# Windowed attention inside a two-layer encoder: the query split moves to the weight-sum tiles, and probabilities, values and unit ends come one step later

## The chip, the cores and the metric

The kernel runs on one core of one Trainium2 chip. The metric is the device time of one execution in microseconds (us). Engines are named as in the profile: PE (TensorE matmul), PEld (TensorE weight load, which runs beside PE), DVE (VectorE), ACT (ScalarE), POOL (GpSimd) and SP (SyncE, which here only issues DMAs).

## What is computed

Two sequences, 512 and 256 tokens of width 1024, go through two layers with the same weights. Each layer is half a SwiGLU network, a token mixer, and half a SwiGLU network again; layer 0 mixes with a gated linear recurrence, layer 1 with windowed attention. The change touches the attention alone:

```python
def window_gqa_mixer(x, w_qkv, w_o, sinks):        # 16 query heads, 4 key heads, head width 64
    q, k, v = split(x @ w_qkv)
    q, k = rope_partial(q), rope_partial(k)
    ...
    s = einsum('bnqhgd,bnkhd->bnhgqk', qb, kband) * d ** -0.5
    s = where(|kpos - qpos| <= 128, s, -inf)
    m = maximum(max(s), sink)
    p = exp(s - m)
    denom = sum(p) + exp(sink - m)
    o = einsum('bnhgqk,bnkhd->bnqhgd', p / denom, vband)
    return o.reshape(B, T, Hq * d) @ w_o
```

## The kernel before

**Numbers in two parts.** Matmuls run on fp32r operands. An fp32 operand is cast to fp32r (the high part, ACT) and the rest is subtracted (the low part, DVE); a product takes three matmuls (lines 261 to 263). `split` (lines 266, 267) does this for activations, lines 167 and 168 for weights.

**Memory.** Large activations live in an arena (`big`, 21 slots of 6 KB per partition). Weights arrive raw in `wr` tiles through the SP queue (line 152) and leave as `w` tiles. Two further tiles, tag `s3`, hold sums of weight blocks for the feed-forward stages: line 186 loads a block into them, line 142 adds another by a POOL-issued DMA. No attention weight uses them. All matmul outputs go to eight PSUM banks (`ps`).

**The attention stage** (`swa`, line 945) lies between the second layer's two feed-forward halves. It first projects keys and values, then runs 24 units: for each of 4 key heads, the 6 blocks of 128 tokens, each with the 4 query heads of that key head. A unit's steps are the methods of `Unit` (line 1107):

- `query`: splits the rotated query block, 128x256, high part on ACT, low part on DVE (lines 266, 267), into a tile `st`
- `turn`: four PE transposes of `st` (line 943) and one ACT copy of the result to SBUF (line 1132)
- `scores`: two matmuls for each of four heads (lines 1141, 1142), each head followed by one DVE instruction that adds the mask and takes the minimum (line 1144)
- `exps`, `sink`, `denominator`: four ACT exponentials (line 1157), small sums (lines 1163, 1164, 1169), a reciprocal (line 1170) and four POOL multiplications that normalize (line 1173)
- `probs(j)`: for each key block j, four PE transposes (line 1179) and a split of the result on ACT and DVE (lines 266, 267, now to `tA` tiles)
- `values(j)`: two matmuls (lines 1191, 1192) that add up in one bank `po`
- `finish`: an ACT copy (line 1197) and two DVE additions (line 1202) that empty `po`

**What sets the order.** `pipeline` (line 1080) gives each of these calls a step number; unit i starts at step 4i. Between them it puts pieces of the query projection, of the output projection (`wo`, lines 261 to 263), and the splits of finished attention outputs (lines 1016, 1017). The calls are recorded in that order, and a scheduler places the instructions on each engine by that order, their data and the tile slots that are free. On the chip each engine then takes its own list strictly in turn.

Of the kernel before, what the change touches and what calls it, by code (L numbers as in the profile page):

```python
# [10 lines left out]
F32R = mybir.dt.float32r  # L11
# [5 lines left out]
P = 128  # L17
# [11 lines left out]
GQ = 4  # L29
# [19 lines left out]
class Trunk:  # L49
# [1030 lines left out]
    def pipeline(self, units, extra):  # L1080
        events = []

        def at(step, rank, *calls):
            events.append((step, rank, len(events), calls))

        for i, u in enumerate(units):
            t = 4 * i
            at(t - (3 if i else 5), 5, u.query)
            at(t - 2, 3.5, u.turn)
            for h in range(GQ):  # L1090
                at(t + h // 2, 0, lambda u=u, h=h: u.scores(h))
            at(t + 2, 2, u.sink)
            for h in range(GQ):
                at(t + 1 + h // 2, 2, lambda u=u, h=h: u.exps(h))
            at(t + 2, 2, u.denominator)
            for j in range(u.nkb):
                at(t + 6 + j, 1, lambda u=u, j=j: u.probs(j))
                at(t + 8 + j, 4, lambda u=u, j=j: u.values(j))
            at(t + 7 + u.nkb, 4, u.finish)
        for step, call in extra:  # L1100
            at(step, 3, call)
        for _, _, _, calls in sorted(events, key=lambda e: e[:3]):
            for c in calls:
                c()


class Unit:
# [12 lines left out]
    def query(self):  # L1120
        k = self.k
        q = self.q().rearrange("p (h d) -> p h d", d=HD)
        self.st = k.big([P, GQ, P], F32R)
        k.split(q, self.st[:, :, :HD], self.st[:, :, HD:])

    def turn(self):
# [190 lines left out]
```

## Time and profile before

| | us |
|---|---|
| median of 3 runs (2806.42 to 2807.36) | 2807.12 |
| the profiled execution's own time | 2808.21 |
| its span in the profile | 2806.4 |
| PE busy | 2775.5 |
| DVE busy | 2161.0 |
| ACT busy | 1329.5 |
| POOL busy | 372.7 |
| attention units on PE, first score to last score | 2089 to 2263 |

The span runs from the first to the last instruction; the remaining 1.8 us lie around it. Matmuls overlap each other, so a busy PE row does not mean that PE starts matmuls as fast as it can.

### The profile page before, as it was taken

How to read it: one execution, taken by the hardware profiler on the slowest of the kernel's cores; microseconds unless marked ns; L12 is line 12 of the kernel's file. 1: busy time of each engine (PE TensorE's matmuls, PEld its weight loads, DVE VectorE, ACT ScalarE, POOL GpSimd, SP SyncE). 2: the span in 40 equal slices, each digit the busy share in tenths (PEclk: the TensorE clock that was granted, in tenths of full speed). 3: DMA queues.
4: the chain of work that ended last, by engine and by line, in shares of the span. 5: the costliest groups of instructions: out<-in, count | busy, mean ns of one | idle time of the engine just before them, and what ended most of it. 6: DMA issues, size and time to landing. Idle time of an engine off the chain costs nothing.

```text
span 2806.4 us, 40557 instructions
## 1 busy us (share of the span) xinstructions
PE 2775.5 (99%) x15225; PEld 2551.2 (91%) x15225; DVE 2161.0 (77%) x3760; ACT 1329.5 (47%) x2455; POOL 372.7 (13%) x402
## 2 busy tenths in 40 slices
PE   8999999999999999999999999999999899999998
PEld 8999999889899889999999999999887789999998
DVE  8788788477577658878878887887848868878877
ACT  6344444444344436434444644444458755444443
POOL 2111121000000001211111111111002211211111
PEclk9999999999999999999999999999999999999999
DMA  6554464311111133555444355554412113555443
GB/s 175 126 130 120 114 145 125 107 46 38 52 40 31 65 94 83 142 126 131 118 116 121 83 143 129 127 120 113 138 69 76 38 47 82 145 134 127 115 118 108
DMA packets 330101, 291.37 MB, mean 104 GB/s; under 512 B 11608, under 2 KB 257840, under 8 KB 329904
## 3 DMA queue, kind: packets, MB, share of 16 engines
q1 hardware_dynamic: 293920, 212.37, 25.5%
q0 software_dynamic: 31680, 62.93, 13.5%
q10 hardware_dynamic: 4304, 13.49, 1.3%
q8 instruction: 119, 1.95, 0.3%
q14 instruction: 78, 0.64, 0.1%
HBM read 216.39 MB, written 9.44 MB: 80 GB/s over the span
## 4 chain that ended last, share of the span: by engine, by line
PE 95%; ACT 2%; DVE 2%; DMA 0%; POOL 0%; issue 0%; DVEq 0%; ACTq 0%; POOLq 0%
PE ps L437 42%; PE ps L501 20%; PE ps L263 8%; PE ps L261 8%; PE ps L262 8%; PE ps L693 3%; PE ps L797 1%; PE ps L773 1%; PE ps L331 1%; PE ps L1179 1%; ACT big L1157 0%; PE ps L1141 0%; POOL big L1173 0%; PE ps L943 0%; PE ps L1192 0%
## 5 line engine op out<-in xcount | busy, mean ns | idle before, releaser
L437 PE MATMUL ps<-big,w 128*128 128x384 f32 x6720 | 1169.3, 334 | 0.0
L437 PEld LDWEIGHTS ps<-big,w 128*128 128x128 f32 x6720 | 1165.9, 188 | 1.7 <-ACT tA L454 0.2
L200 ACT CAST w<-wr 128x512 fp32r<-128x512 f32 x600 | 417.1, 707 | 680.8 <-PE ps L437 273.3
L501 PE MATMUL ps<-w,big 128*128 128x512 f32 x2520 | 575.3, 389 | 0.0
L501 PEld LDWEIGHTS ps<-w,big 128*128 128x128 f32 x2520 | 472.7, 188 | 97.5
L201 DVE TENSOR_TENSOR w<-wr,w 128x512 fp32r<-128x512 f32 (+1 forms) x520 | 429.6, 830 | 157.8 <-ACT w L200 133.4
L523 DVE SCALAR_TENSOR_TENSOR x<-ps,x 128x512 f32<-128x512 f32 x468 | 301.9, 683 | 10.0 <-PE ps L263 9.9
L142 POOL DMA_DIRECT2D s<-wr x120 | 104.9, 874 | 1504.5 <-DMA wr<-in_ffn_w_dram 646.9
L261 PE MATMUL ps<-w,big 128*128 128x512 f32 x624 | 250.0, 401 | 0.3
L263 PE MATMUL ps<-w,big 128*128 128x512 f32 x624 | 245.2, 393 | 2.1 <-DVE big L1017 1.1
L262 PE MATMUL ps<-w,big 128*128 128x512 f32 x624 | 244.5, 392 | 0.0
L261 PE MATMUL ps<-big,w 128*128 128x384 f32 (+2 forms) x640 | 220.1, 345 | 2.1 <-DVE big L339 1.1
L262 PE MATMUL ps<-big,w 128*128 128x384 f32 (+2 forms) x640 | 216.1, 338 | 0.2
L263 PE MATMUL ps<-big,w 128*128 128x384 f32 (+2 forms) x640 | 215.3, 336 | 0.0
L266 ACT CAST big<-tA 128x384 fp32r<-128x384 f32 x296 | 148.1, 513 | 112.8 <-DVE tA L476 36.2
L267 DVE TENSOR_TENSOR big<-tA,big 128x384 fp32r<-128x384 f32 x296 | 168.2, 579 | 6.7 <-ACT big L266 4.5
L168 DVE TENSOR_TENSOR w<-wr,w 128x1024 fp32r<-128x1024 f32 x92 | 111.8, 1221 | 78.0 <-ACT w L167 72.7
L201 POOL TENSOR_TENSOR w<-wr,w 128x512 fp32r<-128x512 f32 x80 | 134.1, 1676 | 187.8 <-ACT w L200 187.5
L167 ACT CAST w<-wr 128x1024 fp32r<-128x1024 f32 x92 | 96.6, 1052 | 108.8 <-PE ps L262 85.8
L142 POOL DMA_DIRECT2D wr<-wr x100 | 87.7, 877 | 420.6 <-DVE w L201 177.5
L263 PEld LDWEIGHTS ps<-w,big 128*128 128x128 f32 x624 | 117.4, 188 | 28.5 <-DVE big L1017 2.0
L261 PEld LDWEIGHTS ps<-w,big 128*128 128x128 f32 x624 | 117.8, 189 | 22.3 <-ACT w L167 0.3
(175 smaller groups left out, 3276.4 us busy)
## 6 DMA issues: line engine op xcount, KB each, us to landing
wr<-in_ffn_w_dram SPq DMA_DIRECT2D x264, 512.0 KB, 3.9
s<-in_ffn_w_dram SPq DMA_DIRECT2D x120, 256.0 KB, 3.2
s<-wr POOLq DMA_DIRECT2D x120, 256.0 KB, 4.8
wr<-wr POOLq DMA_DIRECT2D x80, 256.0 KB, 3.8
wr<-in_hg_w_in_dram SPq DMA_DIRECT2D x40, 512.0 KB, 3.7
wr<-wr POOLq DMA_DIRECT2D x20, 512.0 KB, 4.6
spill<-x ACTq DMA_DIRECT2D x12, 512.0 KB, 3.3
x<-spill ACTq DMA_DIRECT2D x12, 512.0 KB, 3.2
```

The lines of the kernel that those rows point to most:

```text
L142: self.nc.gpsimd.dma_start(out, src, accum_op=ALU.add)
L168: self.nc.vector.tensor_sub(lo, raw, hi.bitcast(F32))
L200: nc.scalar.copy(h, src)
L201: (eng or nc.vector).tensor_sub(l, src, h.bitcast(F32))
L261: nc.tensor.matmul(out, a[0], b[0], start=first, stop=False)
L262: nc.tensor.matmul(out, a[0], b[1], start=False, stop=False)
L263: nc.tensor.matmul(out, a[1], b[0], start=False, stop=last)
L266: self.nc.scalar.copy(hi, src)
L267: self.nc.vector.tensor_sub(lo, src, hi.bitcast(F32))
L437: self.nc.tensor.matmul(ps, a[x], b[y], start=first and k == 0 and i == 0, stop=k == 3 and i == 2, skip_group_check=True,)
L501: nc.tensor.matmul(ps, a[x], w[y], start=name == chain and kp == 0 and q == 0, stop=kp == 1 and q == 2, skip_group_check=True,)
L523: self.nc.vector.scalar_tensor_tensor(x, ps, c, x, ALU.mult, ALU.add)
```

## The change

Two edits. The tile for the split query comes from the two `s3` tiles, each 512 columns, in place of an arena slot. And in the table of steps, `probs`, `values` and `finish` of each unit move one step later against everything else.

```diff
             for j in range(u.nkb):
-                at(t + 6 + j, 1, lambda u=u, j=j: u.probs(j))
-                at(t + 8 + j, 4, lambda u=u, j=j: u.values(j))
-            at(t + 7 + u.nkb, 4, u.finish)
+                at(t + 7 + j, 1, lambda u=u, j=j: u.probs(j))
+                at(t + 9 + j, 4, lambda u=u, j=j: u.values(j))
+            at(t + 8 + u.nkb, 4, u.finish)
...
-        self.st = k.big([P, GQ, P], F32R)
+        st = k.wp.tile([P, 512], F32R, tag="s3", name=k.name("s3"), bufs=2)
+        self.st = st.rearrange("p (h d) -> p h d", d=P)
         k.split(q, self.st[:, :, :HD], self.st[:, :, HD:])
```

Since a line is added, lines from 1124 on are numbered one higher in the changed kernel (scores 1142 and 1143, probabilities 1180, values 1192 and 1193).

What this does to the engines' lists shows at three places. The first is the DVE list around the low part of unit 21's query (it reads `big_19580`, the rotated queries). Before, it stands behind unit 18's `finish` (L1202), unit 19's first probability split (which writes `tA_20380`) and a weight split (L168):

```order
L1163 TENSOR_TENSOR stat_20329<-stat_20327,nsinks 128x4
L168 TENSOR_TENSOR w_20359<-wr_19809,w_20358 128x1024
L1202 TENSOR_TENSOR big_20368<-ps_20338,tA_20366 64x2x128 x2
L267 TENSOR_TENSOR tA_20380<-ps_20374,tA_20379 128x512
L267 TENSOR_TENSOR big_20371<-big_19580,big_20371 128x4x64
L1169 TENSOR_TENSOR stat_20328<-stat_20328,stat_20329 128x4
L521 TENSOR_TENSOR x_19544<-ps_20351,x_19544 128x512
```

In the changed kernel the same subtraction writes the `s3` tile (printed as `s_3093_20364`):

```order
L1170 TENSOR_TENSOR stat_20139<-stat_20139,stat_20140 128x4
L1171 RECIPROCAL stat_20139<-stat_20139 128x4
L1203 TENSOR_TENSOR big_19806<-ps_20175,tA_20207 64x2x128 x2
L267 TENSOR_TENSOR tA_20217<-ps_20211,tA_20216 128x512
L267 TENSOR_TENSOR s_3093_20364<-big_19580,s_3093_20364 128x4x64
L1145 ISA big_20227,stat_20228<-ps_20231,big_17955,nsinks 128x384
```

There it stands behind unit 16's `finish` and unit 17's first probability split, and ahead of unit 19's first scores: two units earlier.

The second place is the PE list at unit 10, from its query transposes (L943) to its first score. Before, one block of unit 8's probability transposes (L1179) lies between them:

```order
L943 MATMUL ps_19348<-ident_r,big_19320 128x128 x4
L1179 MATMUL ps_19361<-ident_r,big_19189 128x128 x4
L1141 MATMUL ps_19374<-big_17959,tA_19353 128x256
L1142 MATMUL ps_19374<-big_17959,tA_19353 128x256
L1141 MATMUL ps_19378<-big_17959,tA_19353 128x256
L1142 MATMUL ps_19378<-big_17959,tA_19353 128x256
```

In the changed kernel the first score (L1142) follows directly behind these twelve rows:

```order
L943 MATMUL ps_19337<-ident_r,s_2835_19318 128x128 x4
L1192 MATMUL ps_19315<-tA_19286,big_17962 128x512
L1180 MATMUL ps_19346<-ident_r,big_19180 128x128 x4
L261 MATMUL ps_19239<-w_18814,big_17871 128x512
L1193 MATMUL ps_19315<-tA_19287,big_17962 128x512
L1192 MATMUL ps_19315<-tA_19309,big_17962 128x512
L262 MATMUL ps_19239<-w_18815,big_17871 128x512
L263 MATMUL ps_19239<-w_18814,big_17871 128x512
L261 MATMUL ps_19239<-w_18814,big_17872 128x512
L1193 MATMUL ps_19315<-tA_19310,big_17962 128x512
L262 MATMUL ps_19239<-w_18815,big_17872 128x512
L263 MATMUL ps_19239<-w_18814,big_17872 128x512
```

Value matmuls of unit 7 (L1192, L1193) and a stretch of projection now stand between the transposes and the scores.

The third place is the PE list at unit 16, again from its query transposes. `big_19732` before, and `big_19723` after, are unit 14's probabilities. Before:

```order
L943 MATMUL ps_19919<-ident_r,big_19885 128x128 x4
L1179 MATMUL ps_19932<-ident_r,big_19732 128x128 x4
L1141 MATMUL ps_19945<-big_17960,tA_19924 128x256
L1142 MATMUL ps_19945<-big_17960,tA_19924 128x256
L1141 MATMUL ps_19949<-big_17960,tA_19924 128x256
L1142 MATMUL ps_19949<-big_17960,tA_19924 128x256
L1179 MATMUL ps_19953<-ident_r,big_19732 128x128 x4
L1191 MATMUL ps_19980<-tA_19893,big_17962 128x512
L1192 MATMUL ps_19980<-tA_19894,big_17962 128x512
L1141 MATMUL ps_19983<-big_17960,tA_19924 128x256
```

In the changed kernel:

```order
L943 MATMUL ps_19908<-ident_r,s_2977_19883 128x128 x4
L1180 MATMUL ps_19917<-ident_r,big_19723 128x128 x4
L1142 MATMUL ps_19936<-big_17960,tA_19913 128x256
L1143 MATMUL ps_19936<-big_17960,tA_19913 128x256
L1142 MATMUL ps_19940<-big_17960,tA_19913 128x256
L1143 MATMUL ps_19940<-big_17960,tA_19913 128x256
L1180 MATMUL ps_19944<-ident_r,big_19723 128x128 x4
L1142 MATMUL ps_19971<-big_17960,tA_19913 128x256
L1143 MATMUL ps_19971<-big_17960,tA_19913 128x256
L1142 MATMUL ps_19975<-big_17960,tA_19913 128x256
L1143 MATMUL ps_19975<-big_17960,tA_19913 128x256
L1180 MATMUL ps_19979<-ident_r,big_19723 128x128 x4
```

Here the row behind the query transposes is still one block of probability transposes, but it is unit 14's first block where it was the second; its first block stood 13 rows ahead of the query transposes before. All four heads' scores now stand with only one such block among them.

On SP the two loads of weight sums for the last feed-forward stage move: before they stand among the loads at the end of the previous feed-forward stage, in the changed kernel behind the last query users of the two tiles, between two pairs of weight loads for the last feed-forward stage. POOL's list keeps its order, and outside the attention stage the lists of PE, DVE and ACT keep theirs.

## The prediction

> **What bounds the kernel now.** I read the page first, then the table of windows through the attention stage, then the waits of PE and PEld there, then the timeline at the longest of them.
>
> ```profile
> span 2806.4 us, 40557 instructions
> PE 2775.5 (99%) x15225; PEld 2551.2 (91%) x15225; DVE 2161.0 (77%) x3760; ACT 1329.5 (47%) x2455; POOL 372.7 (13%) x402
> PE 95%; ACT 2%; DVE 2%; DMA 0%; POOL 0%; issue 0%; DVEq 0%; ACTq 0%; POOLq 0%
> ```
>
> The chain that ended last is PE for 95% of the span, and neither edit adds or removes a matmul. So only time in which PE stands still, or is kept from starting its next matmul, can come back. The windows (columns: length, then busy time of PE, PEld, DVE, ACT, POOL, then the granted clock of PE) show where that is inside the units:
>
> ```profile
> 2100.00:2120.00 20.00, 18.89 (x109) 16.27 (x108) 15.41 (x43) 15.44 (x37) 5.70 (x11) 1.00 0.20 67
> 2120.00:2140.00 20.00, 19.46 (x107) 15.16 (x107) 16.75 (x59) 15.80 (x46) 6.50 (x13) 1.00 0.19 67
> 2140.00:2160.00 20.00, 19.49 (x114) 16.44 (x112) 15.10 (x53) 15.36 (x44) 5.30 (x10) 1.00 0.22 79
> 2160.00:2180.00 20.00, 19.96 (x117) 16.36 (x118) 16.01 (x58) 16.03 (x46) 5.53 (x12) 1.00 0.16 54
> 2180.00:2200.00 20.00, 17.90 (x100) 14.34 (x99) 17.83 (x50) 16.83 (x44) 8.10 (x12) 1.00 0.15 51
> 2200.00:2220.00 20.00, 16.86 (x94) 12.79 (x93) 17.88 (x55) 16.11 (x44) 3.67 (x8) 1.00 0.16 56
> 2240.00:2260.00 20.00, 17.86 (x99) 14.78 (x98) 16.77 (x47) 14.59 (x40) 4.89 (x8) 0.91 0.18 54
> ```
>
> PE is idle for 1.11 + 0.54 + 0.51 + 0.04 + 2.10 + 3.14 + 2.14 = 9.6 us. No other engine is full: DVE, the busiest, reaches 35.7 of 40 us from 2180 to 2220. So the units are held by order, by who stands behind whom, and not by work. The waits between 2080 and 2270 (who waited for whom: us in total, times, longest):
>
> ```profile
> PE ps L943 <- DVE big L267: 3.2, 3, 1.9
> PE ps L1141 <- ACT tA L1132: 2.5, 6, 1.3
> PE ps L1179 <- POOL big L1173: 2.2, 3, 1.3
> PE ps L263 <- DVE big L1017: 1.1, 1, 1.1
> ...
> PEld ps L1141 <- ACT tA L1132: 6.3, 12, 1.5
> PEld ps L1179 <- POOL big L1173: 4.8, 10, 1.5
> ```
>
> The PE rows are full stops, and add up to 9.0 us. The PEld rows count more: a late weight load also delays its matmul while an older one still drains, but a load that is a little late costs nothing. So each cost lies between its two rows.
>
> **The sum, term by term.** To see what a move does I count, in the printed lists, the PE work that stands between an event and the matmul that needs it. The spacing of matmuls is from the timeline:
>
> ```profile
> 2086.14 0.45 PE L943 MATMUL ps<-ident_r,big 128*128 128x128 f32 x4
> 2086.43 0.46 PE L261 MATMUL ps<-w,big 128*128 128x512 f32 x1
> ...
> 2089.03 0.39 PE L263 MATMUL ps<-w,big 128*128 128x512 f32 x1
> 2089.26 0.28 PE L1141 MATMUL ps<-big,tA 128*128 128x256 f32 x1
> 2089.38 0.28 PE L1142 MATMUL ps<-big,tA 128*128 128x256 f32 x1
> ```
>
> That is 0.29 us for four transposes, 0.23 for a matmul of 512 columns, 0.12 for one of 256; I take 0.17 for 384, between them.
>
> *Query transposes that wait for the split query: 3.2 us, all gained.* The longest is unit 21's:
>
> ```profile
> 2241.12 0.39 ACT L266 CAST big<-big 128x256 fp32r<-128x256 f32 x1
> 2241.95 0.42 DVE L267 TENSOR_TENSOR big<-big,big 128x256 fp32r<-128x256 f32 x1
> 2242.43 0.53 PE L943 MATMUL ps<-ident_r,big 128*128 128x128 f32 x4 [1.87 <-DVE big L267]
> ```
>
> The split reaches PE just in time when nothing disturbs it, since it stands behind other units' ACT and DVE work that itself waits for PE. In the DVE lists, the PE work between the last matmul that anything ahead of the split needs and the transposes themselves is 3.2 us on average over the 24 units and 1.4 at least (unit 21); in the changed list it is 7.2 and 3.6. The split takes 0.39 + 0.42 us. I see nothing late in its place: the second query tile holds, since every split stands behind the transposes two units earlier that free it.
>
> *The clock: 1.7 us, gained with unit 21's wait.* One-microsecond windows behind that wait:
>
> ```profile
> 2241.00:2242.00 1.00, 0.00 (x0) 0.00 (x0) 0.97 (x3) 1.00 (x4) 0.00 (x0) 1.00 0.15 44
> ...
> 2244.00:2245.00 1.00, 1.00 (x9) 1.00 (x8) 1.00 (x3) 0.13 (x1) 1.00 (x2) 0.73 0.00 0
> 2245.00:2246.00 1.00, 1.00 (x4) 0.81 (x4) 0.81 (x5) 0.78 (x2) 1.00 (x3) 0.50 0.43 129
> 2246.00:2247.00 1.00, 1.00 (x3) 0.78 (x3) 1.00 (x2) 1.00 (x3) 0.37 (x1) 0.50 1.13 326
> 2247.00:2248.00 1.00, 1.00 (x4) 0.76 (x3) 1.00 (x4) 1.00 (x5) 0.00 (x0) 0.57 0.28 81
> ```
>
> The clock falls to half soon after the stop and costs 0.27 + 0.50 + 0.50 + 0.43 = 1.7 us. No other window above is under 1.00, and the dip follows the longest stop, so I let it go with it. The Trainium skill, page "TensorE: Matmul & The Clock Gate", section "What's actually happening", lets the clock fall only after an idle window of about 3.4 us, in windows that run freely. This trace disagrees: the stop was 1.87 us. By the page the dip would not hang on this stop, and the sum below would be 1.7 us smaller; I follow the row.
>
> *Probabilities that wait for POOL's normalization: 3.5 us gained, of 2.2 to 4.8.* This is what the later step is worth. From a unit's last score to its first probability transpose stand 7.1 us of PE work on average now (4.4 at least), 9.2 in the changed list (6.2 at least). The chain that must fit is softmax input, exponentials, reciprocal and four normalizations. No wait of this kind is longer than 1.5 us, and two more microseconds cover that for nearly all units; I take the middle of the two rows.
>
> *Scores that wait for the copied query: 2.0 us gained, of 1.2 to 5.0.* From the start of the transposes at 2242.43 to the score that used the copy, 1.26 us passed with a short queue:
>
> ```profile
> 2243.69 0.39 PE L1141 MATMUL ps<-big,tA 128*128 128x256 f32 x1 [0.27 <-ACT tA L1132]
> ...
> 2203.56 0.39 PE L1141 MATMUL ps<-big,tA 128*128 128x256 f32 x1 [1.28 <-ACT tA L1132]
> ```
>
> Less the 0.29 us of transposes, 0.97 us of PE work has to stand between. Seven units have less now, four in the changed list (12, 13, 16, 17). The longest wait, 1.28 us, is unit 16's, and its list is no better there (third place above), so I leave it in: 2.5 - 1.3 = 1.2 us at least, 6.3 - 1.3 = 5.0 at most, and 2.0 since the PE row is the surer one.
>
> *New: waits for a PSUM bank, 2.0 us lost, of 0 to 4.5.* A unit's end one step later keeps its bank `po` longer, and all eight score matmuls of a unit now often stand with a single block of transposes among them. Counting banks that are written but not yet read, at five places (units 5, 6, 8, 10, 16) the ninth bank is asked for just as the first is due back; no place before is that tight. Banks are freed by DVE's softmax input:
>
> ```profile
> L1144 DVE CUSTOM_DVE_ANT_0 big<-ps,big,nsinks 128x256 f32<-128x256 f32 (+1 forms) x96 | 47.5, 523 | 16.3 <-PE ps L1142 15.2 <-POOL big L1173 0.8
> ```
>
> Four of these take 2.1 us, while PE is through the scores and the block in 8 x 0.12 + 0.29 = 1.2. The difference, 0.9 us, five times over is 4.5 us; no PE row shows such a wait now, which speaks for 0. I take a little under half. What is queued behind such a wait is all of PE.
>
> *New: the output projection that waits for DVE, 1.0 us lost, of 0 to 2.0.* The 1.1 us behind L1017 stay, since that split does not move. Ahead of it PE now loses this to unit 14's probabilities:
>
> ```profile
> 2197.66 0.33 PE L1179 MATMUL ps<-ident_r,big 128*128 128x128 f32 x1 [1.27 <-POOL big L1173]
> 2198.90 0.33 PE L1179 MATMUL ps<-ident_r,big 128*128 128x128 f32 x1 [0.68 <-POOL big L1173]
> ```
>
> If PE comes to the projection earlier by these 1.3 + 0.7 us, the wait grows by as much at most; I take half of it.
>
> *Moved loads: 0.*
>
> ```profile
> 1990.44 0.37 SPq L186 DMA_DIRECT2D s<-in_ffn_w_dram  x1
> ...
> 2275.67 19.33 SPq L152 DMA_DIRECT2D wr<-in_ffn_w_dram  x4
> ...
> 2297.40 0.92 POOL L142 DMA_DIRECT2D s<-wr  x1 [26.32 <-issue]
> ```
>
> ```profile
> s<-in_ffn_w_dram SPq DMA_DIRECT2D x120, 256.0 KB, 3.2
> ```
>
> Two weight-sum loads, one of them here at 1990, must now wait for the transposes of units 22 and 23, at about 2255. The loads queued behind them on SP left at 2275 and the sum was added at 2297, so 20 us of slack hide them. Without that cover it would be one such transfer, 3.2 us.
>
> Sum: -3.2 - 1.7 - 3.5 - 2.0 + 2.0 + 1.0 = -7.4 us. Against the profiled execution (2808.2 us, its span 2806.4 and 1.8 around it) that is 2800.8; that execution lies 1.1 above the median, so from the median 2807.1 it is **2799.7 us**.
>
> **Rivals.** *The waits change places.* Gains at their low ends (3.2 + 2.2 + 1.2 = 6.6), the clock dips anyway after some other stop, PSUM takes 4.5: -2.1 us, 2805.0. For it: DVE and ACT keep their work, and from 2120 to 2180, where units 5 to 11 stand, PE is idle for 1.1 us in all, so a bank wait there may eat all that they gain. Against it: the stops of units 3 and 21, where most of the 3.2 us lies, have nothing to do with banks.
>
> *PSUM sets the pace, and the kernel gets slower.* If the bank asked for is always one that the same unit's softmax input frees, every unit from 5 on pays 0.9 us: 19 x 0.9 = 17 us, against 8.3 gained with the clock (6.6 + 1.7): +8.8, 2816. It decides from the point where nine banks are live in most units. I count that in five of 24, so it is unlikely.
>
> *The query split does not go early*, because its two tiles are still held. Then 3.2 and 1.7 are not gained: 2804.6. The printed list speaks against it.
>
> **How the numbers follow.** The forecast has 0.62, the change of places 0.27, the slower case 0.07, the held tiles 0.04. All costs at their good ends give -3.2 - 1.7 - 4.8 - 5.0 = -14.7, more than PE's idle time and the dip together (9.6 + 1.7 = 11.3; the rest is in PEld's rows alone), so I end the range between them, 13 us down, at 2794. The other end takes in the changed places with both new costs at their worst: -6.6 + 4.5 + 2.0 = -0.1, 2807. A measurement of this kernel tells about 0.2% from no change, 5.6 us. The forecast's own spread, 2794 to 2803.5, lies below 2801.5 for some nine tenths: faster 0.56, same 0.36, slower 0.08.
>
> **What would show it.** Right: no PE row for L943 behind DVE's L267; the clock at 1.00 from 2240 to 2260; the POOL row under 1 us; the wait of L1142 (now the score's line) down to one long piece near unit 16; the whole gain between 2100 and 2260, the rest of the kernel equal. Wrong: PE or PEld rows that wait for DVE's L1145 or L1203, which free banks; a new dip of the clock; DVE above 18 of 20 us in the windows around 2200, with the wait behind L1017 at 3 us; or a loss behind 2275, where the weight sums come late.

## The result, and the profile after

The changed kernel takes 2799.33 us (median of 9 runs, 2799.10 to 2800.37); the kernel before, run beside it on the same chip, takes 2807.12 us (9 runs, 2806.34 to 2807.74). The ratio is 0.9974, interval [0.9964, 0.9984]: faster by 7.8 us, where 7.4 were forecast. The profiled execution has a span of 2797.3 us, 9.1 less than before; that is more than 7.8 because the profiled execution of before was a long one (2808.21 us, 1.1 above its median) and the one after a little short (2799.13). From here on the lines of the changed kernel from 1124 on stand one higher than those of before: scores L1142 and L1143, softmax input L1145, probabilities L1180, values L1192 and L1193, a unit's end L1203.

The head of the page after:

```profile
span 2797.3 us, 40580 instructions
PE 2772.5 (99%) x15225; PEld 2553.0 (91%) x15225; DVE 2159.4 (77%) x3760; ACT 1329.7 (48%) x2455; POOL 369.2 (13%) x402
PE 96%; DVE 2%; ACT 1%; DMA 0%; issue 0%; DVEq 0%; ACTq 0%; SPq 0%
```

PE still carries the chain. The same windows as before (length, busy time of PE, PEld, DVE, ACT, POOL, granted clock of PE):

```profile
2100.00:2120.00 20.00, 19.26 (x112) 16.25 (x110) 17.37 (x46) 16.25 (x39) 7.19 (x12) 1.00 0.28 90
2120.00:2140.00 20.00, 19.13 (x111) 16.22 (x111) 15.53 (x56) 15.18 (x45) 5.55 (x12) 1.00 0.30 96
2140.00:2160.00 20.00, 20.00 (x122) 17.20 (x121) 16.18 (x58) 17.34 (x49) 6.41 (x12) 1.00 0.16 54
2160.00:2180.00 20.00, 19.89 (x118) 16.88 (x116) 17.23 (x63) 16.47 (x49) 5.55 (x12) 1.00 0.09 27
2180.00:2200.00 20.00, 17.55 (x99) 14.37 (x98) 17.37 (x48) 18.34 (x44) 4.56 (x8) 0.96 0.17 56
2200.00:2220.00 20.00, 19.55 (x109) 16.12 (x108) 18.05 (x62) 15.63 (x46) 5.54 (x12) 0.95 0.15 52
2240.00:2260.00 20.00, 20.00 (x115) 17.13 (x115) 17.91 (x54) 14.73 (x43) 5.55 (x12) 1.00 0.17 51
```

In these seven windows PE is now idle for 0.74 + 0.87 + 0 + 0.11 + 2.45 + 0.45 + 0 = 4.6 us, where it was 9.6. In the last of them, 2240 to 2260, no idle time is left, and the clock is at 1.00. But 2180 to 2220 now has a clock under 1.00 that it did not have. The waits of PE between 2080 and 2270, all of them, and the larger ones of PEld:

```profile
PE ps L1193 <- DVE tA L267: 1.9, 1, 1.9
PE ps L1180 <- DVE tB L939: 0.7, 1, 0.7
PE ps L1142 <- ACT tA L1133: 0.7, 2, 0.5
PE ps L1192 <- ACT tA L266: 0.6, 1, 0.6
PE ps L261 <- DVE big L1203: 0.2, 1, 0.2
PE ps L943 <- DVE s L267: 0.2, 1, 0.2
```

```profile
PEld ps L1193 <- DVE tA L267: 3.2, 4, 2.3
PEld ps L1142 <- ACT tA L1133: 1.8, 4, 0.7
```

Two rows of before are gone (POOL's normalization, the projection behind L1017), two are nearly gone (the query transposes 3.2 to 0.2, the scores 2.5 to 0.7), and a new one stands on top: values that wait for the low half of the split probabilities, one stop of 1.87 us. This is where it comes from:

```profile
2192.58 1.22 DVE L168 TENSOR_TENSOR w<-wr,w 128x1024 fp32r<-128x1024 f32 x1
2193.71 1.96 DVE L1017 TENSOR_TENSOR big<-big,big 128x512 fp32r<-128x512 f32 x4
...
2196.39 0.69 DVE L267 TENSOR_TENSOR tA<-ps,tA 128x512 fp32r<-128x512 f32 x1
...
2197.14 0.50 PE L1193 MATMUL ps<-tA,big 128*128 128x512 f32 x1 [1.87 <-DVE tA L267]
```

DVE takes a weight split (L168), the four output splits of heads group 0 (L1017) and two softmax inputs (L1145, not shown) ahead of the low split that PE needs; it is busy without a gap from 2192 to 2197. And behind this stop lies the clock dip that had stood at 2244:

```profile
2198.00:2199.00 1.00, 0.53 (x6) 0.30 (x4) 1.00 (x2) 1.00 (x4) 0.00 (x0) 0.74 0.00 0
2199.00:2200.00 1.00, 1.00 (x5) 1.00 (x6) 1.00 (x3) 0.94 (x2) 0.00 (x0) 0.50 0.15 41
2200.00:2201.00 1.00, 1.00 (x6) 1.00 (x5) 0.99 (x4) 0.00 (x0) 0.30 (x1) 0.50 0.86 305
2201.00:2202.00 1.00, 1.00 (x8) 1.00 (x7) 0.97 (x4) 0.90 (x2) 1.00 (x3) 0.55 0.70 242
```

It costs 0.26 + 0.50 + 0.50 + 0.45 = 1.7 us, as before: the dip has moved, and was not removed.

Where in the program the gain lies is read from the first transposes behind the stage (L331):

```profile
L331 PE MATMUL ps<-ident_r,big x42: 270/272/329, 2305.5 to 2318.0; 128*128 128x128 f32 x42
```

```profile
L331 PE MATMUL ps<-ident_r,big x48: 270/272/308, 2296.5 to 2313.0; 128*128 128x128 f32 x48
```

These are before and after. The stage ends 9.0 us earlier, of the span's 9.1; 0.7 of that was there already at the stage's first score (2089.3 against 2088.6), and it is there by about 27 us from the kernel's start, in a part whose lists the edits leave as they were. The late weight sums cost nothing behind 2275. So all but 0.7 us of the gain lies in the attention stage, as forecast, and the question left is which edit made it.

### The profile page after: what moved, and what is told of

It reads as the page before. It is cut to its first block, busy times and chain, and to the rows that moved or that the text cites. A ratio compares the mean times of both kernels' runs of the same rounds, so it can differ in the third digit from the quotient of the medians.

```text
span 2797.3 us, 40580 instructions
## 1 busy us (share of the span) xinstructions
PE 2772.5 (99%) x15225; PEld 2553.0 (91%) x15225; DVE 2159.4 (77%) x3760; ACT 1329.7 (48%) x2455; POOL 369.2 (13%) x402
## 4 chain that ended last, share of the span: by engine, by line
PE 96%; DVE 2%; ACT 1%; DMA 0%; issue 0%; DVEq 0%; ACTq 0%; SPq 0%
PE ps L437 42%; PE ps L501 20%; PE ps L261 9%; PE ps L263 9%; PE ps L262 9%; PE ps L693 3%; PE ps L797 1%; PE ps L1180 1%; PE ps L773 1%; PE ps L331 1%; PE ps L1142 0%; PE ps L1143 0%; PE ps L1192 0%; PE ps L1193 0%; PE ps L943 0%; DVE x L523 0%
## 5 line engine op out<-in xcount | busy, mean ns | idle before, releaser
L266 ACT CAST big<-tA 128x384 fp32r<-128x384 f32 x296 | 148.0, 513 | 114.2 <-DVE tA L476 36.2
L168 DVE TENSOR_TENSOR w<-wr,w 128x1024 fp32r<-128x1024 f32 x92 | 111.6, 1220 | 75.8 <-ACT w L167 70.4
```

Source lines behind the costliest of these rows:

```text
L168: self.nc.vector.tensor_sub(lo, raw, hi.bitcast(F32))
L266: self.nc.scalar.copy(hi, src)
```

## The experiments

The waits count only full stops. For a finer sum I add up, over all matmuls of the stage (2080 to 2285), what the distance from one start to the next has beyond the 0.225 us that 512 columns take undisturbed (others in proportion), where it is more than 0.06 us. This delay, the clock dip in it, is 25.1 us before and 16.2 after: 8.9 us less, close to the span's gain of 9.1. Each run below has a time, a ratio to the kernel before on the same chip, and this delay.

**1. The query tiles alone.** The changed kernel, with the steps of before.

```diff
-                at(t + 7 + j, 1, lambda u=u, j=j: u.probs(j))
-                at(t + 9 + j, 4, lambda u=u, j=j: u.values(j))
-            at(t + 8 + u.nkb, 4, u.finish)
+                at(t + 6 + j, 1, lambda u=u, j=j: u.probs(j))
+                at(t + 8 + j, 4, lambda u=u, j=j: u.values(j))
+            at(t + 7 + u.nkb, 4, u.finish)
```

> The changed kernel with the old steps: only the query split's tile differs from the kernel before. Theory (each edit removes its own wait): the three stops of the query transposes behind the split, 3.2 us, go, since the split stands 7.7 us of PE work ahead of them in the list in place of 3.2; the clock's dip at 2244 goes with the longest of them, 1.7 us. The wait of the probability transposes for the normalization stays near its 2.2 us of PE. Time: 2807.1 - 4.9 = 2802.2 us, or 2803.9 if the clock dips at another stop. Rival (the later step is what wins, the tile only makes room for it): within 2 us of the kernel before, 2805 to 2809.

Measured: 2805.01 us (2803.23 to 2805.67) against 2807.98, ratio 0.999 [0.9981, 0.9999], delay 20.5 us. PE's waits:

```profile
PE ps L1142 <- ACT tA L1133: 3.6, 4, 1.7
PE ps L1180 <- POOL big L1174: 2.1, 3, 1.3
PE ps L263 <- DVE big L1017: 1.1, 1, 1.1
PE ps L943 <- DVE s L267: 0.2, 1, 0.2
```

The query transposes no longer wait, but PE's rows fall by 2.0 us only (9.0 to 7.0) and not by their 3.0: at unit 21 the stop moves to the next thing that this unit needs, the copied query (the row of the scores has grown from 2.5 to 3.6).

```profile
2240.27 0.39 PE L1142 MATMUL ps<-big,tA 128*128 128x256 f32 x1 [1.68 <-ACT tA L1133]
```

The clock is at 1.00 in every window of this run, after a stop of 1.68 us. So the tiles alone are worth 3.0 us by the medians (0.3 to 5.3 by the interval). The profiled span, 2801.4, is 5.0 below that of before, and 1.7 of these 5.0 are the dip; but the profiled execution is the fastest of the eleven, 1.8 us below their median, so whether the others are without the dip is not shown. The expected 2802.2 is not reached: each edit does not simply remove its own wait.

**2. The steps alone.** The kernel before with the three new step numbers, the query split still in the arena (the same three lines, the other way round).

> The later steps with the query split left in the arena. Theory: the wait of the probability transposes (2.2 us of PE, 4.8 of the weight loads) goes, since 9.7 us of PE work stand ahead in place of 7.1; the stops of the query transposes (3.2 us) and a dip of the clock (1.7) stay; the scores' wait for the copied query grows, since 11 units have under 0.97 us of cover in place of 7, by 4 x 0.3 = 1.2 us. Time: 2807.1 - 3.5 + 1.2 = 2804.8 us. Rival (later steps hold arena slots longer, and the split then waits for a slot): slower than before, 2808 to 2812, with the row of L943 over 4 us.

Measured: 2807.97 us (2807.28 to 2810.66), ratio 1.0003 [0.9994, 1.0012], delay 25.8 us: no gain at all, where 2804.8 was expected. Its waits have the line numbers of before:

```profile
PE ps L1192 <- DVE tA L267: 4.0, 2, 2.1
PE ps L1141 <- ACT tA L1132: 2.3, 6, 0.7
PE ps L943 <- DVE stat L1163: 1.1, 2, 0.8
PE ps L1179 <- ACT tA L266: 0.7, 1, 0.7
PE ps L943 <- DVE big L267: 0.6, 2, 0.4
```

The later step does what the prediction said of it: the POOL row is gone. In its place the values wait for the low split, 2.11 us at 2202.87 and 1.89 us at 2250.01. Ahead of both stand four L1017, of 1.96 us, and two softmax inputs in DVE's queue; and each of the two stops is followed by a dip (0.28 + 0.50 + 0.50 + 0.42 from 2203 to 2207; 0.39 + 0.50 + 0.50 + 0.31 from 2251 to 2255), which the 0.91 of these windows show:

```profile
2200.00:2220.00 20.00, 17.22 (x90) 13.26 (x89) 18.18 (x58) 16.20 (x46) 3.84 (x9) 0.91 0.23 79
2240.00:2260.00 20.00, 18.00 (x98) 14.90 (x97) 16.90 (x47) 14.15 (x41) 5.10 (x8) 0.91 0.18 54
```

So -3.0 us for the one and 0.0 for the other, and -7.8 together: some 4.8 us are there only when both edits are. The three intervals reach 2.5 to 2.8 us to each side, together some 4.5 for this surplus, so by the times alone it is only just clear of nothing. The delays of the three profiled executions say the same as the medians: if the edits simply added, 20.5 + 25.8 - 25.1 = 21.2 us would be left, and it is 16.2. The printed lists say what the pair has that neither has alone. Counted as in the prediction, the PE work between a unit's last score and its first probability transpose is 7.1 us on average before, 7.1 with the tiles alone, 9.7 with the steps alone, 9.2 with both. Between the probability transposes and the values that use them it is 3.4, 3.5, 2.6 and 3.1: the steps alone take 0.8 us from the values to give it to the probabilities, and the tiles give 0.5 of it back. Units that have under 0.97 us between the query transposes and their scores: 7, 5, 11 and 4. That these covers are the cause is read from the lists and fits the waits; no run changed one of them alone. Nor does a run tell apart the two things that the tiles edit does: the query is split earlier, and the arena slot that it held is left to other tiles.

**3. Output split of group 0 three steps earlier.** From here on every edit but run 5's is made to the changed kernel. This one takes the four L1017 from the head of the stop at 2197.

```diff
-        extra.append((60, lambda: split_out((0,))))
+        extra.append((57, lambda: split_out((0,))))
```

> The changed kernel with the split of the first key head's outputs at step 57 in place of 60: on DVE the four subtractions L1017 stand ahead of unit 13's first probability split, in place of right ahead of its third. Theory (the stop of 1.87 us at unit 13's values is this order, and the clock's dip behind it, 1.7 us, follows the stop): both go, 2799.3 - 3.6 = 2795.7 us, clock 1.00 from 2180 to 2220. Rival 1 (the dip does not hang on this stop): 2797.5 us with a dip elsewhere. Rival 2 (DVE is full here, and the stop moves to another instruction): 2798.5 to 2800 us, a stop of over 1 us elsewhere between 2180 and 2215.

Measured: 2798.05 us (2797.70 to 2799.25), ratio 0.9967 [0.9955, 0.998], delay 14.6 us. The stop at 2197 shrinks to 0.87 us and the clock is at 1.00 everywhere, but another stop of 0.87 us opens at 2198. The expected 2795.7 was not reached: of 1.9 + 1.7 us some 1.3 came, which is nearer to the second rival (the stop moves to another instruction).

**4. Two steps later instead of one.**

```diff
-                at(t + 7 + j, 1, lambda u=u, j=j: u.probs(j))
-                at(t + 9 + j, 4, lambda u=u, j=j: u.values(j))
-            at(t + 8 + u.nkb, 4, u.finish)
+                at(t + 8 + j, 1, lambda u=u, j=j: u.probs(j))
+                at(t + 10 + j, 4, lambda u=u, j=j: u.values(j))
+            at(t + 9 + u.nkb, 4, u.finish)
```

> The changed kernel with probabilities, values and unit ends two steps later than before, in place of one. Theory (one step already covers the normalization everywhere, so a second has nothing to win, and banks and tiles are held longer): no row of the probability transposes behind POOL in either; 2799 to 2802 us. Rival (the units are still held by that latency): 2795 to 2798 us.

Measured: 2800.18 us (2798.72 to 2800.73), ratio 0.9973 [0.9962, 0.9983], delay 16.5 us. No POOL row here either: one step was enough for it. Now the query transposes (2.4 us, once) and the projection behind L1017 (2.1 us, once) are late, each with its dip. So here other consumers are late, and the time is nearly the same.

**5 and 6. One PSUM bank fewer, before and after.** A bank is written ahead of the units and read behind them; this adds one transpose and one copy.

```diff
-        self.pipeline(list(units(range(KV))), extra)
+        hold = self.ps(P); self.transpose_r(hold, self.identr); self.pipeline(list(units(range(KV))), extra); nc.scalar.copy(self.tmp(P), hold)
```

> The kernel before, with one of the eight PSUM banks held through the attention stage (one more transpose ahead of it and one more copy behind it, well under 1 us in all). Theory (banks are tight only in the changed order): with seven banks the printed lists of before ask for a bank in the last moment at about 4 places out of 234, so 0 to 1.5 us are lost, 2807.1 to 2809. Rival (banks are tight in any order, every unit pays the 0.9 us of one round of softmax inputs): 24 x 0.9 = 20 us, near 2828. Second rival (banks are irrelevant in both kernels): 2807.5 here and no loss in the changed kernel either.

> The changed kernel with one PSUM bank held through the attention stage, as in the run on before. Theory (the later step uses up the spare banks; with eight it loses the 1.0 us that the trace shows): with seven banks some 19 places of the printed lists ask for a bank in the last moment, in about six units; these cost 4.3 us by the lists' own times, so about 2803.6 (2801 to 2806), with PE waits behind L1145 and L1198 or L1203 of 3 us or more. Rival (banks have room in the changed order too, and the 1.0 us is something else): under 1 us lost, 2799 to 2800.5.

Measured: before with seven banks 2809.18 us, ratio 1.0006 [0.9996, 1.0015], against 2807.96 with eight; after with seven 2801.18 us, ratio 0.9976 [0.9967, 0.9986]. Against the changed kernel's 0.9974 that is 0.6 us more by the ratios, 1.9 by the medians, not the 4.3 that the lists gave; neither loss is clear of the intervals. The waits of run 6:

```profile
PE ps L1193 <- DVE tA L267: 2.1, 2, 1.9
PE ps L1142 <- DVE tB L939: 1.0, 1, 1.0
PE ps L1192 <- ACT s L266: 0.5, 1, 0.5
PE ps L1142 <- ACT tA L1133: 0.3, 1, 0.3
PE ps L943 <- DVE stat L1164: 0.3, 1, 0.3
```

Not one PE row waits for the softmax input L1145, which frees the banks of the scores. The 2801.2 us alone would lie at the edge of the theory's range, but the waits of 3 us that were to make it are missing, so my theory of tight banks fell: where a bank comes just in time by the list, no stop is seen here, even with one bank less. What remains is single places (L939 at 2119, 0.7 us with eight banks, 1.0 with seven).

**7 and 9. The output splits spread out.** Run 7 has group 0 at step 36 and group 1 at step 57; run 9 has group 0 at 36 and leaves group 1 at 65.

```diff
-        extra.append((60, lambda: split_out((0,))))
-        extra.append((65, lambda: split_out((1,))))
+        extra.append((36, lambda: split_out((0,))))
+        extra.append((57, lambda: split_out((1,))))
```

> The changed kernel with the output splits of heads group 0 at step 36 (was 60) and of group 1 at step 57 (was 65): the same eight L1017, out of the place where DVE is full. Theory (what is left at 2197 is a backlog of DVE: two weight sums, four output splits and softmax inputs ahead of a low split that PE waits for, and the clock dip hangs on that stop): DVE has 2 x 1.96 us less to do between 2180 and 2220, where it is busy for 35.4 of 40 us; no stop over 1 us is left there, no dip; 2799.3 - 1.9 - 1.7 = 2795.7, and below the 2798.05 of the variant that only moved group 0 by three steps. Rival (every stop that is taken away is made up one step further on, as when group 0 was moved by three steps): 2797.5 to 2799, the clock again under 1.00 in one window.

> The changed kernel with the output split of heads group 0 at step 36 (was 60), where DVE has room, and group 1's left at 65. Theory (what is left to win around 2197 is DVE's backlog there): between about 2185 and 2197 DVE has 1.96 us less ahead of the low splits than in the changed kernel, and also 1.96 less than in the variant with the splits at steps 36 and 57, whose second split came due just there; so no stop over 0.5 us from 2190 to 2200, no dip: 2799.3 - 1.9 - 1.7 = 2795.7 (2795.0 to 2797.0). Rival (the weight sums and softmax inputs alone fill DVE there): stops of about 1 us as in the variants that moved a split, 2798.

Measured: 2798.25 us, ratio 0.9966 [0.9953, 0.9979], delay 14.6 us, and 2798.81 us, ratio 0.9966 [0.9954, 0.9978], delay 15.6 us. In both the clock is at 1.00 throughout, in both the stops at 2197 are 1 us or less, and neither reaches 2795.7. By the time the rival held in both; the dip that it expected in run 7 did not come. Run 9 from 2180 to 2220:

```profile
2180.00:2200.00 20.00, 19.14 (x110) 15.58 (x109) 17.37 (x49) 17.90 (x44) 4.54 (x9) 1.00 0.18 59
2200.00:2220.00 20.00, 18.97 (x108) 14.99 (x107) 18.05 (x62) 15.92 (x47) 5.51 (x12) 1.00 0.14 48
```

DVE is as busy here as in the changed kernel (17.37 + 18.05 in both), although four of its instructions left: the place that had been freed is filled by what comes next, since DVE is behind. From 2192 to 2208 it is busy for 15.92 us of 16 in run 9 (15.96 in the changed kernel); in run 7 it is 14.85, so a DVE without gaps is not what holds run 7. And what PE does not lose at 2197 it has lost elsewhere: by the same weight split (L168) run 9 is 1.6 us later than the changed kernel. The four L1017 now run at 2154.86, and the values and scores behind them start 0.39 and 0.56 us late, at 2157 and 2158; 0.3 us more was there already at the stage's first score (2088.9 against 2088.6). Run 9 makes up for that without the stop and the dip.

```profile
2187.22 1.22 DVE L168 TENSOR_TENSOR w<-wr,w 128x1024 fp32r<-128x1024 f32 x1 [0.46 <-ACT w L167]
```

```profile
2188.81 1.23 DVE L168 TENSOR_TENSOR w<-wr,w 128x1024 fp32r<-128x1024 f32 x1 [0.47 <-ACT w L167]
```

(The first is the changed kernel, the second run 9.)

**8. Output split of group 0 one step later.** The four L1017 now stand behind the low split instead of ahead of it; nothing else moves on DVE. (The edit is 60 to 61.)

> The changed kernel with the output split of heads group 0 one step later (61, was 60), which puts its four L1017 (1.96 us on DVE) behind the low split of unit 13's third probabilities instead of ahead of it; nothing else on DVE moves. Theory (the 1.87 us stop is these four instructions in that place): the stop at 2197 falls under 0.5 us, the clock stays at 1.00 from 2198 to 2202, other waits of up to 1 us for the next low splits (units 14) come in its place: 2796.5 to 2798.0. Rival (DVE's amount of work decides, not its order, so a stop as long comes within the next units, with its dip): 2799 to 2800.

Measured: 2799.73 us (2798.73 to 2800.45), ratio 0.9971 [0.996, 0.9982], delay 16.1 us: the rival's number. The stop at the values is gone, and the next thing behind the four L1017 has it, a query transpose, with the dip behind it again.

```profile
2195.80 1.96 DVE L1017 TENSOR_TENSOR big<-big,big 128x512 fp32r<-128x512 f32 x4
...
2197.68 0.42 DVE L267 TENSOR_TENSOR s<-big,s 128x256 fp32r<-128x256 f32 x1
...
2198.15 0.53 PE L943 MATMUL ps<-ident_r,s 128*128 128x128 f32 x4 [1.71 <-DVE s L267]
```

So the place of the four instructions decides who stops here. That somebody stops because DVE's queue is long fits these runs, but no run made it shorter.

**10 to 12. Idle instructions on DVE.** Run 3's kernel with 6, 8 or 11 instructions more for DVE at step 38 (the band mask's maximum with itself, which changes nothing). They were to make stops of a chosen length, as a test of what the clock dip hangs on.

```diff
+        extra += [(38, lambda: nc.vector.tensor_tensor(self.band[:, :384], self.band[:, :384], self.band[:, :384], ALU.max))] * 11
```

> The variant with group 0's split three steps earlier (the clock at 1.00 in every window of the stage), with 6 idle DVE instructions at step 38 (the band mask's maximum with itself, 128x384, some 0.4 us each: 2.4 us in all), where nothing else is near: no weight sum, no output split, little DMA. It makes PE stop for a time of my choosing. Theory (the dip follows a stop of PE longer than some 1.7 us, whatever makes it): the cover there is 1 to 1.5 us, so a stop of about 1.2 us, no dip, near 2799. Rival (the dips at 2198 come from what runs there, with DVE, ACT and DMA full): no dip here either, and none in the two runs beside this.

> As the run with 6 idle DVE instructions, with 8 (3.3 us). Theory: a stop of about 2 us, and if it is over 1.7 the clock at half for some 3.4 us beginning within 3 us of its end (1.7 us lost): near 2801.5. Rival (the dips come from what runs around 2198): the same stop, the clock at 1.00.

> As the run with 6 idle DVE instructions, with 11 (4.5 us). Theory: a stop of about 3 us, a dip of 1.7 us behind it, no longer than behind a stop of 1.9: near 2803. A third theory (the dip grows with the stop): more than 2.5 us lost to the clock here. Rival (the dips come from what runs around 2198): the stop without a dip.

Measured: 2799.56, 2799.49 and 2800.15 us, ratios 0.997 [0.9957, 0.9982], 0.9969 [0.9956, 0.9982] and 0.9973 [0.9962, 0.9983]. They failed as a test of the clock: the program's order put the instructions between DVE's others, one at a time, so no stop of PE at this place was longer than 0.8 us, and no dip was to be seen. They did give something else. The eleven are 6.0 us of DVE work (0.55 us each, where 0.4 had been expected):

```profile
L1030 DVE TENSOR_TENSOR big<-big x11: 531/549/691, 2156.1 to 2164.8; 128x384 f32<-128x384 f32 x11
```

and the kernel is 2.1 us slower than run 3 by the medians, 1.7 by the ratios: about a third of what is added to DVE here reaches the end, and the rest goes into its gaps. The intervals of the two runs overlap, so the third is a rough figure.

## Why the prediction was right

The forecast was 2799.7 us, and 2799.3 came; the direction, the sum and the stage were right. The terms were less so, and their errors cancel: that the two numbers lie only 0.4 us apart is in good part luck. Of the prediction's own signs, two for being right came (the clock at 1.00 from 2240 to 2260, no POOL row) and so did two for being wrong: a new dip, and DVE above 18 of 20 us from 2200 to 2220 (18.05). By the forecast's own steps:

- *What bounds it: PE, by order and not by work.* Right before the change. After it this is open: from 2192 to 2208 DVE has no gap worth the name (15.96 of 16 us, 14.06 before), so there work may hold it, and the runs that only reordered it (3, 7, 8, 9) end within 1.7 us of each other. But in the two fastest of them, 3 and 7, DVE has gaps in that place (15.25 and 14.85).
- *Query transposes, -3.2 us.* Right as a row (3.2 to 0.2). But by itself it is not worth that: with the tiles alone the scores' row grew by 1.1 us, since the copied query is the next step of the same unit.
- *The clock, -1.7 us.* The mechanism held, the gain did not. The dip did go with the stop at 2242 (with the tiles alone a stop of 1.68 us is left there, and no dip), but I priced it as if no new stop would come, and a new stop of 1.87 us took it over. Here the term was 0.
- *Probabilities behind POOL, -3.5 us.* The wait is gone, more thoroughly than I said (no row at all). But run 2 shows no gain from it without the tiles: the values behind it wait in its place.
- *Scores behind the copied query, -2.0 us.* PE's row fell by 1.8, PEld's by 4.5: the size was right or too small. The place was wrong: I kept a piece of 1.28 us near unit 16, and no wait of this kind is now longer than 0.5.
- *PSUM banks, +2.0 us.* Half of that: 0.7 behind L939 and 0.2 behind L1203. The five places where a score's bank came back just in time cost nothing, and runs 5 and 6 show that even seven banks hardly do.
- *Projection behind L1017, +1.0 us.* Wrong in sign: the wait of 1.1 us went. I let PE come earlier and left L1017 in place; in fact the four instructions of group 0 now hold up a low split first. That what PE loses there it need not lose at the projection is my reading; no run tests it.
- *Not in the forecast: the values behind the low split, +1.9 us* in PE's row, and 0.6 us in the row of the other half (L266). I counted the cover of four waits and not of this fifth, although the list shows it shrink from 3.4 to 3.1 us, and L1017 ahead of it was in view.
- *Moved loads, 0.* Right: the stage's end and the span moved by the same 9 us.

So PE's rows went from 9.0 to 4.3 us, a gain of 4.7, and the delays that are no full stop gave the rest of the 8.9; I had 8.7 of gains and 3.0 of losses in waits, and 1.7 for the clock. The clock that was not gained and the values that were not foreseen (3.6 us) stand against the projection (2.1), the banks (1.0), and the scores' late starts that are no full stop.

Of the rivals, the change of places was nearest in kind: waits did change places, as runs 1, 2 and 8 show one by one. It was wrong on the price (2805.0 us), because the waits that came were shorter than those that went.

What stays open is whether a lower limit than 2798 can be reached by order. Runs 3, 7 and 9 are the fastest (2798.05, 2798.25, 2798.81), but their intervals and that of the changed kernel overlap, so none is shown to beat it. That DVE is the next bound around 2200 is suggested by the runs and not shown; a run that takes work off DVE there was not made.

## What to carry to other kernels

When a wait is taken away, ask for every later wait of the same unit how much work covers it in the new order, and price the first that is thin: two edits that each gain little can gain together, by these lists because each supplies the cover that the other uses up. In these traces a clock dip belongs to a long stop, so its price moves with the longest stop that is left, and is gained only when no such stop is left. Where an engine's rows run almost without a gap, moving its work about mostly changed who waits for it.

## What the runs showed of the hardware

In the profiled executions of all these runs a stop of PE of 1.71 us or more in the stage was followed by the half clock, and one of 1.68 us or less was not. The stops with a dip, by their waits: 1.87 (before), 1.87 (after), 2.11 and 1.89 (run 2), 2.42 and 2.07 (run 4), 1.87 (run 5), 1.90 (run 6), 1.71 (run 8). Without one: 1.68, 1.27, 1.27 and 1.10 (run 1), 1.28, 1.27, 1.13 and 1.11 (before), and all those of about 1 us in runs 3, 7 and 9 to 12. Each dip loses 1.7 us in all, that is 3.4 us at half clock, however long the stop was, and it begins between 0.1 us ahead of the stop's end (run 4) and 2.1 us behind it.

Where a dip begins is set by a grid that the stop has no part in. The clock records of the trace of before hold full clock for 2232.317 us, half for 3.413 and full for 552.959, which is 654, 1 and 162 times 3.4133 us; in all fourteen traces the stretches of full clock are such whole multiples. So a dip is one step of this grid, and it begins at the first grid point at the stop's end or behind it. In the step that ends there, PE is idle for 1.58 us (run 5) to 2.32 us (run 4). Steps with no dip behind them have up to 1.68 us (run 1) and 1.66 (before, 2196.67 to 2200.08, from two stops); the next has 1.51. So idle time of 1.88 us or more in a step always brought a dip and 1.51 or less never did; in between both are seen.

The Trainium skill, page "TensorE: Matmul & The Clock Gate", section "What's actually happening", gives windows of about 3.4 us that run freely; the length of the dips and the grid agree with this, but by the page an idle window must pass first, and no stop here was near 3.4 us. Whether the length of one stop counts, with a threshold near 1.7 us, or the idle time in a step of the grid can't be settled from these nine dips: both fit, and the three runs that were to set the length of the stop did not make one. If the grid decides, another execution of the same kernel can have the same stop without the dip, since the grid falls elsewhere; there is one trace of each kernel.
